# A hybrid decoder layer on one core: eight pairs of projection tiles by Strassen's form, attention's two chains side by side, first tiles by depth

## The chip, the cores and the metric

The kernel runs on one core of one Trainium2 chip. The metric is the device time in microseconds of one execution of the whole program; of several executions the median is given. One execution was recorded by the hardware profiler, and every row below is from it.

## The reference, cut to what matters

One layer over 1024 tokens of width 1024, all in 32-bit floats:

```python
h = rmsnorm(x, norm_in_g)
proj = h @ w_in            # 1024 x 4784, cut into eleven parts
(cq, ckv, kr, gate_mla, gq, gk, gv, gk_low, gate_gla, merge_a, merge_b) = split_in(proj)
...                        # latents cq (384) and ckv (256): rmsnorm, then queries, keys and values
o_mla = mla_attention(...) # 8 heads, causal softmax
y_a = (o_mla * silu(gate_mla)) @ w_mla_br
o_gla = gla_chunked(qg, kg, vg, log_a)   # 4 heads, a decaying state along the tokens
y_b = (rmsnorm(o_gla) * silu(gate_gla)) @ w_gla_br
merged = sigmoid(merge_a) * y_a + sigmoid(merge_b) * y_b
x = x + merged @ w_out
e = rmsnorm(p @ w_ple, ple_norm_g)
x = x + sigmoid(rmsnorm(x, ple_gate_norm_g) @ w_ple_gate) * e
out = rmsnorm(x, final_norm_g)
```

## The kernel before, in words

**Products.** Each 32-bit operand is cut into a high half that TensorE takes in its reduced format and a low half with the rest (`split`, lines 126 to 128: ScalarE writes the high half, VectorE the low one). One product is three matmuls, high by high, high by low and low by high (`mm3`, lines 144 to 147). A *bank* (`bank`, line 149) is one PSUM bank of 128 output features by 512 tokens: eight tiles of depth 128, three matmuls each, 24 matmuls of 512 columns; then an eviction scales it by the tokens' reciprocal norms `rb`.

**Streams.** `stream` (line 158) is a generator over weight tiles of 128 features. Each tile is loaded by SyncE into a slot, split, used for two banks (the two halves of the tokens), and dropped; the next tile is fetched when the first bank of the present one begins. All tiles of 128 by 1024 live in 35 slots, later 39, handed out in the order in which they became free.

**Order of the work.** The program is written as nested generators, and a scheduler orders each engine's instructions by the program's order and by which operands it expects to be ready; on the chip every engine runs its own list in order. The stages around the change:

1. *First tiles* (lines 298 to 350). The input comes transposed in eight tiles of depth (`xT`), is split into `xh` and `xl`, and squared for the norm. The mixed tile (`w0`: rotary keys and the low-rank gate) and four tiles of linear attention's queries and keys (`first`) are computed bank after bank. Six PSUM banks "d" and two "u" serve this stage. `rb` is known only after all eight tiles of the input.
2. *Values, gate and rotary tables.* Eight banks of values (`gv`), with the decay `bt` and the rotary tables `cs` and keys `krt` on VectorE and ScalarE beside them.
3. *Linear attention* (`gla(t, h)`, line 529) in four chains, two pairs of heads `t` by two halves of the tokens `h`. A chain has eleven steps: state updates (0), six levels of decay tiles with their cross products (1 to 6; `level`, line 533), the last level (7), the output (8), its norm (9), and the product with the gate (10). The chains run one after the other, and after every step one bank of `fill` is issued: a stream over 29 tiles of the projection, four of GLA's gate, four of MLA's gate, eight and eight of the merge gates, two and three of the latents. Its evictions scale (lines 466, 471), apply tanh and write to DRAM or keep the result.
4. *Latents and branch.* `finish_latent` (line 756) norms a latent: squares summed by TensorE, a Newton iteration of small VectorE operations, a broadcast by TensorE, scaling and splitting. The small latent is finished within `fill`, the large one later, and 16 half-size banks of the branch product `yb` fill around them, before the value products and softmax attention.
5. Softmax attention, output products, embedding and the final norm, which the change touches only where they read `krt` and `cs`.

## Time and profile before

| | us |
|---|---|
| time, median of three runs | 984.45 (983.88 to 986.28) |
| profiled execution, its own time | 983.49 |
| profiled execution, span from first to last instruction | 981.7 |
| TensorE busy in the span | 955.8 (5216 matmuls) |
| VectorE busy | 590.2 |
| ScalarE busy | 413.1 |
| GpSimd busy | 128.1 |

The span leaves out what lies before the first and after the last instruction. Busy times of the engines overlap. Matmuls are pipelined and their ends are modelled, so the distance between two starts, not the duration of one, is what a matmul costs in a stream. PE is TensorE, DVE VectorE, ACT ScalarE, POOL GpSimd, SP SyncE; L12 is line 12 of the program.

### The profile page before, as it was taken

What the parts mean: (1) busy time and instruction counts of PE and PEld (TensorE: products, weight loads), DVE (VectorE), ACT (ScalarE), POOL (GpSimd) and SP (SyncE); (2) the same over time, 40 slices, a digit from 0 to 9 for tenths busy, and PEclk for the clock granted to TensorE, in tenths of its full rate; (3) what the DMA queues carried; (4) which work ended last, traced back from release to release, by engine and by line L of the source; (5) the groups of instructions that cost most, each with busy time, mean ns of one, the idle gap of its engine ahead of it and who ended that gap; (6) DMA issues with size and microseconds to landing.
All of it is one profiled execution on the core that took longest, in us unless ns stands there. A gap on an engine that the chain in (4) does not pass through costs nothing.

```text
span 981.7 us, 14101 instructions
## 1 busy us (share of the span) xinstructions
PE 955.8 (97%) x5216; PEld 794.3 (81%) x5216; DVE 590.2 (60%) x1227; ACT 413.1 (42%) x800; POOL 128.1 (13%) x103
## 2 busy tenths in 40 slices
PE   7999999999999999999999999997999999999995
PEld 5887877887887887888888778886888788889985
DVE  6737765574474474433476469785757863239666
ACT  7306731331331342321333257676885432228333
POOL 2100000000000000001101012235363000000422
PEclk9999999999999999999999999997999999999998
DMA  7200211122222122211253844537146761136112
GB/s 281 94 22 22 65 43 43 57 84 86 76 108 86 63 79 86 97 65 43 82 181 127 230 121 121 133 98 177 49 147 229 254 208 65 49 119 188 53 69 103
DMA packets 47828, 105.70 MB, mean 108 GB/s; under 512 B 6736, under 2 KB 9616, under 8 KB 47760
## 3 DMA queue, kind: packets, MB, share of 16 engines
q1 hardware_dynamic: 47760, 104.81, 33.1%
q8 instruction: 41, 0.67, 0.3%
q14 instruction: 27, 0.22, 0.1%
HBM read 72.18 MB, written 25.20 MB: 99 GB/s over the span
## 4 chain that ended last, share of the span: by engine, by line
PE 86%; DVE 6%; ACT 3%; DMA 3%; issue 2%; SPq 0%; DVEq 0%; ACTq 0%
PE d L145 19%; PE d L147 18%; PE d L146 18%; PE pt L963 3%; PE pg L147 3%; PE pg L146 3%; PE pg L145 3%; PE L L559 2%; PE o L955 2%; PE s L146 2%; PE o L954 2%; PE s L147 2%; PE s L145 2%; PE o L690 1%; DMA kl<-kl 1%
## 5 line engine op out<-in xcount | busy, mean ns | idle before, releaser
L145 PE MATMUL d<-xh,wh 128*128 128x512 f32 x544 | 215.9, 400 | 2.8 <-ACT xh L132 2.6
L146 PE MATMUL d<-xl,wh 128*128 128x512 f32 x544 | 214.5, 395 | 0.1
L147 PE MATMUL d<-xh,wl 128*128 128x512 f32 x544 | 213.3, 393 | 0.1
L145 PEld LDWEIGHTS d<-xh,wh 128*128 128x128 f32 x544 | 103.0, 190 | 28.1 <-ACT xh L132 4.6
L127 ACT ACTIVATE wh<-wr 128x1024 fp32r<-128x1024 f32 (+4 forms) x81 | 76.2, 943 | 114.3 <-DMA wr<-in_w_in 40.4
L146 PEld LDWEIGHTS d<-xl,wh 128*128 128x128 f32 x544 | 103.0, 189 | 21.9 <-DVE xl L133 0.8
L147 PEld LDWEIGHTS d<-xh,wl 128*128 128x128 f32 x544 | 102.7, 189 | 21.9 <-DVE wl L128 0.5
L128 DVE TENSOR_TENSOR wl<-wr,wh 128x1024 fp32r<-128x1024 f32 (+2 forms) x59 | 74.6, 1267 | 71.2 <-ACT wh L127 71.1
L145 PE MATMUL pg<-wh,gh 128*128 128x256 f32 (+1 forms) x200 | 62.7, 314 | 0.0
L146 PE MATMUL pg<-wl,gh 128*128 128x256 f32 (+1 forms) x200 | 62.5, 313 | 0.0
L147 PE MATMUL pg<-wh,gl 128*128 128x256 f32 (+1 forms) x200 | 62.5, 313 | 0.0
L128 DVE TENSOR_TENSOR pt<-pt,pt 128x512 fp32r<-128x512 f32 (+1 forms) x96 | 51.4, 550 | 17.1 <-ACT pt L127 16.9
L494 ACT ACTIVATE z<-z 128x512 f32<-128x512 f32 x32 | 20.2, 631 | 98.0 <-DVE z L466 94.2
L924 ACT ACTIVATE p<-p,nm 128x128 f32<-128x128 f32 (+3 forms) x64 | 49.3, 772 | 21.2 <-DVE nm L914 21.1
L466 DVE TENSOR_TENSOR z<-d,rb 128x512 f32<-128x512 f32 x32 | 22.1, 690 | 51.3 <-PE d L147 51.3
L127 ACT ACTIVATE pt<-pt 128x512 fp32r<-128x512 f32 (+1 forms) x96 | 44.6, 485 | 15.5 <-PE pt L963 13.6
L145 PE MATMUL d<-mh,wh 128*128 128x512 f32 x128 | 50.7, 399 | 0.0
L146 PE MATMUL d<-ol,wh 128*128 128x512 f32 x128 | 50.1, 392 | 0.4 <-DVE ol L128 0.4
L147 PE MATMUL d<-mh,wl 128*128 128x512 f32 x128 | 50.2, 392 | 0.0
L147 PE MATMUL d<-oh,wh 128*128 128x512 f32 x128 | 50.1, 391 | 0.0
L146 PE MATMUL d<-ml,wh 128*128 128x512 f32 x128 | 49.9, 390 | 0.0
L145 PE MATMUL d<-oh,wh 128*128 128x512 f32 x128 | 49.9, 395 | 0.0
(263 smaller groups left out, 1924.4 us busy)
## 6 DMA issues: line engine op xcount, KB each, us to landing
wr<-in_w_in SPq DMA_DIRECT2D x33, 512.0 KB
d_ta<-z SPq DMA_DIRECT2D x16, 256.0 KB
d_tb<-z SPq DMA_DIRECT2D x16, 256.0 KB
tb<-d_tb SPq DMA_DIRECT2D x16, 256.0 KB
d_zb<-tb SPq DMA_DIRECT2D x16, 256.0 KB
d_e<-er SPq DMA_DIRECT2D x16, 256.0 KB
ta<-d_ta SPq DMA_DIRECT2D x16, 256.0 KB
zb<-d_zb SPq DMA_DIRECT2D x16, 256.0 KB
```

What stands on the lines that cost most here:

```text
L127: nc.scalar.activation(dst_hi, src, AF.Copy)
L128: (eng or nc.vector).tensor_tensor(dst_lo, src, f(dst_hi), op=ALU.subtract)
L145: nc.tensor.matmul(ps, lh, rh, start=first, stop=False)
L146: nc.tensor.matmul(ps, lh, rl, start=False, stop=False)
L147: nc.tensor.matmul(ps, ll, rh, start=False, stop=last)
L466: nc.vector.tensor_tensor(z, ps, rb[:, hs(h)], op=ALU.mult)
L494: nc.scalar.activation(z, z, AF.Tanh, scale=0.5)
L559: nc.tensor.matmul(L[:, hd * HALF + c * P : hd * HALF + (c + 1) * P], lt[rows(hd), cs], rt[rows(hd), cs], start=True, stop=True,)
L924: nc.scalar.activation(pt[:, :w], pt[:, :w], AF.Exp, bias=nm, scale=-1.0, accum_out=den)
L954: nc.tensor.matmul(po[:, n0:], vv, ts_[:, n0:HALF], start=kb == 0, stop=False)
L955: nc.tensor.matmul(po[:, n0:], vv, ts_[:, HALF + n0 : S], start=False, stop=kb == nk - 1)
L963: nc.tensor.transpose(pt[:, j * P : (j + 1) * P], pq[j][:, kb * P : (kb + 1) * P], ident)
```

## The change

**Pairs of tiles by a Strassen product** (the form with seven products and fifteen additions). 16 of the 29 tiles leave the stream: three of the first merge gate, all eight of the second, and the five latent tiles. They are taken in eight pairs. For a pair the weights are a 2 by 2 matrix of blocks (tile by half of the depth), the input another (half of the depth by half of the tokens). Seven products, each of four depth tiles and three matmuls of 512 columns, replace eight such. Sums of input blocks (`tq`) are made once, sums of weight blocks per pair on GpSimd, and the products are combined by accumulating twice into a bank and by additions on VectorE in the evictions. The input's four blocks now lie in tiles that hold high and low half side by side (`xq`).

**Linear attention's chains** run side by side: the two halves of pair 0 are one chain of 22 steps, those of pair 1 another, which starts seven steps later. In 29 rounds 22 banks of the remaining 13-tile stream are issued. One bank goes ahead of the rounds; the last three are issued in the next PSUM pool, around the input's sums.

**First tiles by depth.** The mixed tile and the two query tiles are computed together: each depth tile of the input goes into six open banks as it arrives. The PSUM pool has seven banks "d" and one "u" for it.

**Memory.** Rotary keys and tables and the finished gates are written to DRAM and loaded again later, the input is loaded a second time for its sums, slots are 34 and later 39, temporaries of 512 columns 8 instead of 6, linear attention's buffers 9 instead of 6. The small latent is finished after the pairs, ahead of the branch product. The DMA scratch of the program is set to 1024 bytes.

```diff
-NSLOT = 35
-NMORE = 4
-NTMP = 6
-NG = 6
+NSLOT = 34
+NMORE = 5
+NTMP = 8
+NG = 9
...
+        def mm3(ps, lh, ll, rh, rl, first, last, more=False):
+            nc.tensor.matmul(ps, lh, rh, start=first, stop=False, skip_group_check=more)
+            nc.tensor.matmul(ps, lh, rl, start=False, stop=False, skip_group_check=more)
+            nc.tensor.matmul(ps, ll, rh, start=False, stop=last, skip_group_check=more)
+        def pair(t):
+            return t[:, 0:HALF], t[:, HALF:S]
...
+        def strassen(get, jobs, xs, ahead=4):
+            raws, sums, ws, st = {}, {}, {}, {}
+            W = HALF
+            order = [(0, j) for j in (0, 4, 6, 1, 2, 3, 5)]
+            order += [(n, j) for n in range(1, len(jobs)) for j in range(7)]
+            def load(n):
+                if n < len(jobs):
+                    raws[n] = [alloc(F32, "wr") for _ in range(2)]
+                    for r, src in zip(raws[n], jobs[n][0]):
+                        nc.sync.dma_start(r, src)
+            def prep(q):
...
+                n, j = order[q]
+                r1, r2 = raws[n]
+                a11, a12, a21, a22 = r1[:, :W], r1[:, W:], r2[:, :W], r2[:, W:]
+                if j == 0:
+                    sums[n] = alloc(F32, "ws")
+                s1, s2 = sums[n][:, :W], sums[n][:, W:]
+                ws[n, j] = alloc(F32R, "sw")
+                if j == 0:
+                    nc.gpsimd.tensor_tensor(s1, a21, a22, op=ALU.add)
+                    nc.gpsimd.tensor_tensor(s2, s1, a11, op=ALU.subtract)
+                    nc.gpsimd.tensor_tensor(a21, a11, a21, op=ALU.subtract)
+                if j == 6:
+                    nc.gpsimd.tensor_tensor(a12, a12, s2, op=ALU.subtract)
+                split(*pair(ws[n, j]), (a11, s2, s1, a21, a12, a22, a12)[j])
+                if q % 7 == 5:
+                    drop(raws[n][n > 0])
+                    load(n + 1)
+                if q % 7 == 6:
+                    drop(*raws.pop(n), sums.pop(n))
+            def run(n, j):
+                b = ("abcbadc" if n else "abcbydx")[j]
+                first = b not in st
+                if first:
+                    st[b] = get("w", "w" + b)
+                hi, lo = pair(ws[n, j])
+                for i in range(4):
+                    c = slice(i * P, (i + 1) * P)
+                    mm3(st[b], hi[:, c], lo[:, c], *pair(xs[j][i]), first and i == 0, i == 3, b in "abc")
+                drop(ws.pop((n, j)))
+                _, ev1, ev2 = jobs[n]
+                def plus(t, b):
+                    nc.vector.tensor_tensor(t, st[b], t, op=ALU.add)
+                if j == 0:
+                    st["e"] = t2("e")
+                    nc.scalar.activation(st["e"], st["a"], AF.Copy)
+                elif j == 1:
+                    st["v"] = t2("v")
+                    nc.vector.tensor_tensor(st["v"], st["b"], st["e"], op=ALU.add)
+                elif j == 3:
+                    w_, z = t2("w"), t2("z22")
+                    st["u"] = w_
+                    nc.vector.tensor_tensor(w_, st["b"], st["e"], op=ALU.add)
+                    nc.vector.tensor_tensor(z, st["c"], w_, op=ALU.add)
+                    ev2(1, z)
+                    if not n:
+                        plus(st["v"], "c")
+                        plus(st["v"], "x")
+                        ev1(1, st["v"])
+                elif j == 4:
+                    if n:
+                        ev1(0, st["a"])
+                    else:
+                        z = t2("z11")
+                        nc.vector.tensor_tensor(z, st["y"], st["e"], op=ALU.add)
+                        ev1(0, z)
+                elif j == 5:
+                    plus(st["u"], "d")
+                    ev2(0, st["u"])
+                elif j == 6 and n:
+                    plus(st["v"], "c")
+                    ev1(1, st["v"])
+                if j == order[7 * n + 6][1]:
+                    st.clear()
...
+            for q, (n, j) in enumerate(order):
+                prep(q + ahead)
+                run(n, j)
...
-            get = psum_pool({"d": (HALF, 6), "u": (HALF, 2)}, ps0)
+            get = psum_pool({"d": (HALF, 7), "u": (HALF, 1)}, ps0)
...
+            w3 = [(alloc(F32, "wr"), alloc(F32R, "wh"), alloc(F32R, "wl")) for _ in range(3)]
+            src3 = [a["w_misc"][:, NVEC : NVEC + S]] + [job(W_GQ + t, None)[0] for t in range(2)]
+            ev3 = [ev_misc, ev_q(0), ev_q(1)]
+            ps3 = [[None, None] for _ in range(3)]
+            def load3(n, c0, c1):
+                raw, hi, lo = w3[n]
+                c = slice(c0, c1)
+                if n == 0 and c0 == 0:
+                    split(hi[:, c], lo[:, c], wm0[:, NVEC : NVEC + c1])
                 else:
+                    nc.sync.dma_start(raw[:, c], src3[n][:, c])
+                    split(hi[:, c], lo[:, c], raw[:, c])
+                if c1 == S:
+                    drop(raw)
...
+            for k in range(8):
+                t = alloc(F32, "xT")
+                for c in (hs(0), hs(1)) if k == 0 else (slice(0, S),):
+                    nc.sync.dma_start(t[:, c], a["xT"][k * P : (k + 1) * P, c])
+                if k == 0:
+                    load3(0, 0, P)
+                for h in range(2):
+                    xq[h].append(alloc(F32R, f"x{h}{k}"))
+                    split_gain(*xin(k, h), t[:, hs(h)], col(V_IN + k))
+                xT.append(t)
+                if k == 0:
+                    load3(0, P, S)
+                    load3(1, 0, 256)
+                    load3(2, 0, 256)
+                if 0 < k < 3:
+                    load3(k, 256, S)
+                if k == 2:
+                    nc.sync.dma_start(ident, a["cst"][:, C_ID : C_ID + P])
+                for n in range(3):
+                    _, hi, lo = w3[n]
+                    for h in range(2):
+                        if k == 0:
+                            ps3[n][h] = get("d", "d")
+                        c = slice(k * P, (k + 1) * P)
+                        mm3(ps3[n][h], hi[:, c], lo[:, c], *xin(k, h), k == 0, k == 7)
+                if k:
+                    square(k - 1)
...
+                nc.sync.dma_start(d_krt, f(krt))
+                for y in range(2):
+                    nc.sync.dma_start(d_cs[y], cs[y])
+                drop(ang, kk, kr, krt, *cs)
...
-                for _ in range(2):
+                for _ in range(2 if tb < 3 else 1):
...
-            jobs += [job(W_MA + m, ev_t(d_ta[m])) for m in range(8)]
-            jobs += [job(W_MB + m, ev_t(d_tb[m])) for m in range(8)]
-            fill = stream(get, jobs, xh, xl)
+            jobs += [job(W_MA + m, ev_t(d_ta[m])) for m in range(5)]
+            order = [(n, h) for n in range(12) for h in range(2)] + [(12, 1), (12, 0)]
+            fill = stream(get_fill, jobs, xin, order=order)
             next(fill)
-            def steps():
+            def chain(t):
                 for h in range(2):
-                    for t in range(2):
-                        yield from gla(t, h)
+                    yield from gla(t, h)
             next(fill)
-            n_left = 2 * len(jobs) - 5
-            for _ in steps():
-                next(fill)
-                n_left -= 1
-            drop(*bt, gci)
+            def load_x(i):
+                raw[i] = [alloc(F32, "xr") for _ in range(2)]
+                for n in range(2):
+                    nc.sync.dma_start(raw[i][n], a["xT"][(i + 4 * n) * P : (i + 4 * n + 1) * P, :])
+            def keep(t):
+                for m in (2 * t, 2 * t + 1):
+                    nc.sync.dma_start(d_sg[m], sg[m])
+                    drop(sg[m])
+                drop(bt[t])
+            one, two, lag = chain(0), chain(1), 7
+            for n in range(22 + lag):
+                if n < 22:
+                    next(one)
+                if n >= lag:
+                    next(two)
+                if n not in (8, 10, 12, 14, 17, 20, 23):
+                    next(fill)
+                if n == 22:
+                    keep(0)
+                    load_x(0)
+                    load_x(1)
...
+        with tc.tile_pool(name="psS", bufs=1, space=PSUM) as psS:
+            get = psum_pool({"d": (HALF, 4), "w": (HALF, 4)}, psS)
+            getF[0] = get
...
+            ts = [tile_of(W_MA + m, ev_t(d_ta[m])) for m in range(5, 8)]
+            ts += [tile_of(W_MB, ev_t(d_tb[0]))]
+            ts += [tile_of(W_CKV + j, ev_ckv(j)) for j in range(2)]
+            ts += [tile_of(W_CQ + j, ev_cq(j)) for j in range(3)]
+            ts += [tile_of(W_MB + m, ev_t(d_tb[m])) for m in range(1, 8)]
+            jobs = [((p_[0], q_[0]), p_[1], q_[1]) for p_, q_ in zip(ts[::2], ts[1::2])]
+            tq = [[], [], [], []]
+            def operand_sums(i):
+                r = raw.pop(i)
+                for n in range(2):
+                    nc.scalar.activation(r[n], r[n], AF.Copy, scale=col(V_IN + i + 4 * n))
+                x11, x12, x21, x22 = (r[n][:, hs(h)] for n in range(2) for h in range(2))
+                for q_ in tq:
+                    q_.append(alloc(F32R, "tq"))
+                nc.gpsimd.tensor_tensor(x11, x12, x11, op=ALU.subtract)
+                nc.vector.tensor_tensor(x12, x22, x12, op=ALU.subtract)
+                nc.gpsimd.tensor_tensor(x22, x22, x11, op=ALU.subtract)
+                nc.vector.tensor_tensor(x21, x21, x22, op=ALU.subtract)
+                for q_, x in zip(tq, (x11, x22, x12, x21)):
+                    split(*pair(q_[i]), x)
+                drop(*r)
+            load_x(2)
+            load_x(3)
+            keep(1)
+            xs = [xq[0][:4], tq[1], tq[0], tq[2], xq[0][4:], tq[3], xq[1][4:]]
+            pairs = strassen(get, jobs, xs)
+            next(fill)
+            operand_sums(0)
+            operand_sums(1)
+            next(fill)
+            operand_sums(2)
+            next(fill)
+            next(pairs)
+            operand_sums(3)
+            drop(*xq[1][:4])
+            next(pairs)
+            for _ in fill:
+                pass
+            for q in range(7 * len(jobs)):
+                next(pairs)
+                j = q - 7 * (len(jobs) - 1)
+                if j >= 0:
+                    drop(*xs[j])
+                if j == 3:
+                    sg = [alloc(F32, f"sg{m}") for m in range(4)]
+                    oh, ol = [], []
+                    for m in range(4):
+                        nc.sync.dma_start(sg[m], d_sg[m])
+                        oh.append(alloc(F32R, "oh"))
+                        ol.append(alloc(F32R, "ol"))
+                        split(oh[m], ol[m], sg[m])
+                        drop(sg[m])
+            drop(rb)
...
-            for n in range(n_left - 5):
-                next(fill)
-            kvh, kvl = finish_latent(get, "u", "L", "ckv", 256, V_KV)
-            next(fill)
-            next(fill)
-            next(fill)
+            kvh, kvl = finish_latent(get, "d", "d", "ckv", 256, V_KV)
...
+            cs = [alloc(F32, "cs") for _ in range(2)]
+            for y in range(2):
+                nc.sync.dma_start(cs[y], d_cs[y])
...
-                    nc.sync.dma_start(f(qk[nm, 2 * pr][64:96]), f(krt[32 * y : 32 * y + 32]))
+                    nc.sync.dma_start(f(qk[nm, 2 * pr][64:96]), d_krt[32 * y : 32 * y + 32])
```

## Rows read from the trace of the kernel before

**Rows 1.** The page's busy times, and TensorE's busy tenths in 40 slices:

```profile
PE 955.8 (97%) x5216; PEld 794.3 (81%) x5216; DVE 590.2 (60%) x1227; ACT 413.1 (42%) x800; POOL 128.1 (13%) x103
...
PE   7999999999999999999999999997999999999995
```

**Rows 2.** The page's chain that ended last, shares by engine:

```profile
PE 86%; DVE 6%; ACT 3%; DMA 3%; issue 2%; SPq 0%; DVEq 0%; ACTq 0%
```

**Rows 3.** Timeline, evictions of two neighbouring banks (start, us, instruction, idle before):

```profile
426.93 0.69 DVE L466 TENSOR_TENSOR z<-d,rb 128x512 f32<-128x512 f32 x1 [2.66 <-PE d L147]
...
432.37 0.69 DVE L466 TENSOR_TENSOR z<-d,rb 128x512 f32<-128x512 f32 x1 [4.75 <-PE d L147]
```

**Rows 4.** Chain of waits in linear attention (start us, us, what):

```profile
129.12 1.09 PE L L559 x16
...
148.37 1.09 PE L L559 x16
155.12 1.09 PE L L559 x16
```

**Rows 5.** Timeline of TensorE at the start, then busy time of that stretch:

```profile
7.65 0.63 PE L147 MATMUL d<-xh,wl 128*128 128x512 f32 x1
10.39 1.22 PE L145 MATMUL d<-xh,wh 128*128 128x512 f32 x2 [2.12 <-ACT xh L132]
...
15.93 0.39 PE L147 MATMUL d<-xh,wl 128*128 128x512 f32 x1
...
4.80:15.70 10.90, 8.50 (x17) 5.42 (x18) 7.32 (x7) 8.72 (x10) 0.00 (x0) 1.00 0.99 375
```

**Rows 6.** Timeline of ScalarE, first half of the scale row:

```profile
47.05 0.60 ACT L342 ACTIVATE rb<-rb 128x512 f32<-128x512 f32 x1 [2.00 <-PE rb L243]
```

**Rows 7.** Groups by line, 118 to 418 us (busy us, mean ns, idle before):

```profile
L128 DVE TENSOR_TENSOR wl<-wr,wh 128x1024 fp32r<-128x1024 f32 x24 | 29.4, 1224 | 30.7 <-ACT wh L127 30.5
L466 DVE TENSOR_TENSOR z<-d,rb 128x512 f32<-128x512 f32 x29 | 20.0, 690 | 43.9 <-PE d L147 43.9
...
L145 PE MATMUL d<-xh,wh 128*128 128x512 f32 x362 | 144.3, 399 | 0.0
```

**Rows 8.** Stretches: busy us (instructions) of PE, PEld, DVE, ACT, POOL; clock, DMA, GB/s:

```profile
118.00:418.00 300.00, 300.00 (x1891) 242.90 (x1889) 164.81 (x308) 93.14 (x188) 12.13 (x16) 1.00 0.21 75
...
200.00:220.00 20.00, 20.00 (x155) 16.15 (x154) 17.96 (x41) 7.62 (x14) 0.83 (x1) 1.00 0.18 66
...
425.00:459.00 34.00, 34.00 (x152) 28.16 (x151) 5.88 (x8) 5.91 (x8) 2.57 (x2) 1.00 0.14 50
672.00:688.00 16.00, 9.81 (x38) 8.70 (x37) 7.49 (x26) 8.81 (x21) 8.54 (x5) 0.58 0.73 190
688.00:704.00 16.00, 16.00 (x92) 13.77 (x91) 11.97 (x33) 12.49 (x28) 4.13 (x4) 1.00 0.12 43
```

**Rows 9.** Timeline of VectorE before the first cross products, fourth level's differences:

```profile
119.83 0.41 DVE L546 TENSOR_TENSOR r<-b 128x256 f32<-128x256 f32 x1
```

**Rows 10.** Timeline of VectorE and GpSimd near 912 us:

```profile
911.54 0.48 DVE L1186 SCALAR_TENSOR_TENSOR x<-et,re,x 128x256 f32<-128x256 f32 x1
...
912.70 1.29 POOL L1216 TENSOR_TENSOR x<-x,fg 128x512 f32<-128x512 f32 x1 [149.00 <-ACT g L1188]
...
912.82 1.46 DVE L1186 SCALAR_TENSOR_TENSOR x<-et,re,x 128x256 f32<-128x256 f32 x1
```

**Rows 11.** Timeline of ScalarE at the stall of 672 us:

```profile
676.00 1.06 ACT L127 ACTIVATE wh<-wr 128x1024 fp32r<-128x1024 f32 x1 [3.63 <-DMA wr<-in_pT]
```

**Rows 12.** Chain of waits and timeline, the two latents, first and last:

```profile
459.53 1.68 PE ss L222 x16
...
475.19 1.28 DVE L128 TENSOR_TENSOR cl<-latents,ch 128x512 fp32r<-128x512 f32 x2
...
495.01 1.68 PE ss L222 x16
...
519.45 0.39 PE L145 MATMUL d<-ch,wh 128*128 128x512 f32 x1
```

126 lines of the change are left out of this document (57 added, 69 removed).

## The prediction, made before the changed kernel ran

> **What bounds the kernel now.** I read the page's busy times and slices first. TensorE has work in 955.8 of 981.7 us, and its slices are full except the first, one near 670 us and the last [rows 1]; the chain that ended last is 86% TensorE [rows 2]. So what counts is the number of matmul steps and the few places where TensorE waits. The timeline gives the step: two neighbouring banks of the input projection are evicted 5.44 us apart (426.93, 432.37) [rows 3], and a bank is 24 matmuls of 512 columns, so 0.2267 us each. In linear attention the chain of waits repeats every 6.75 us (148.37, 155.12): one bank and 1.31 us for one step's own products [rows 4]. TensorE is full there, VectorE has 164.8 of 300 us [rows 8]. The profiled execution took 983.49 us, 0.96 below the median; I sum against it and add 0.96.
>
> **The change, part by part.**
>
> *Strassen.* 16 of the 29 streamed tiles go in 8 pairs. Before, a pair is 4 banks, 4 x 5.44 = 21.76 us. After, 7 products of 12 matmuls, 7 x 2.72 = 19.04 us. The matmuls keep their form (128x128 weights, 512 columns, new weights each time), so I price them by the same step: 8 x 2.72 = **21.8 us less**. What hides the additions: per pair VectorE gets 7 low halves of 512 columns (0.69 each, as an eviction of that size [rows 3]) and nine operations on the products' sums (five additions, four scalings), 16 x 0.69 = 11.0 us, where two tiles now cost two splits of 1.22 and four evictions, 5.2 [rows 7]; ScalarE gets 7 high halves, a copy and four activations, 12 x 0.60 = 7.2 [rows 6]; GpSimd four weight sums of 1.29 us [rows 10], 5.2. All lie inside 19.04 us of TensorE, in a stretch in which VectorE now works 5.9 of 34 us [rows 8]. GpSimd slows VectorE: while one of its operations runs, a VectorE operation that takes 0.48 takes 1.46 us [rows 10]; even 11.0 + 5.2 fits. It adds one kind of wait: banks a, b and c are accumulated into a second time, and the first of those matmuls waits until VectorE or ScalarE has read the first sum, which it has one product (2.72 us) or more to do. Behind that matmul stand all later products on TensorE, and behind those the evictions; a reader that is late by one GpSimd operation costs up to 1. From 0 to 8 us over 8 pairs, I take **1**, since the cover is wide.
>
> The Trainium skill (TensorE: Matmul & The Clock Gate, section Back-to-back issue gap) gives about 131 ns a matmul for a sustained stream of weight loads and matmuls of 512 columns. By it the 96 matmuls would be 12.6 us and the total some 9 us higher; the row's 226.7 ns differs, and decides.
>
> *Entry.* Four operand sums, each over two input tiles: ScalarE 8 scalings x 1.06 and 16 high halves x 0.60, 18.1 us [rows 6, 11]; of 16 differences and 16 low halves 24 on VectorE, 24 x 0.69 = 16.6, and 8 on GpSimd, 8 x 1.29 = 10.3, during which VectorE can be held. With three evictions and four weight parts (7 x 0.69 = 4.8) VectorE may need 31.7 us. The cover is three banks (16.3) and the three first products, which need no sum (8.2): 24.5. So 0 (part done under the last steps of attention, or on time) to 7.2 us late; I take **2**, because load and first two sums can start under five banks of attention's tail. The saves of finished gates (four of them, two tiles per chain) wait on SyncE for VectorE's last gate product; queued behind them are the input's reload and the next tile's weights, due two banks (10.9 us) later, so a wait of that size is free.
>
> *Attention's two chains.* Before, 44 steps each carry a bank; after, 29 rounds carry 22 banks, up to two steps each, and rounds 8, 10, 12, 14, 17, 20, 23 carry none. No TensorE work is added; cover is lost. Per chain of 11 steps (four of them before): TensorE 300 us less 1086/24 = 45.25 banks (362 matmuls in each of three lines [rows 7]) x 5.44 = 53.8, so 13.5; VectorE 164.8 less the stream's own 71.6 (24 splits of 1.22, 29 evictions of 0.69, and for 16 banks of gates two such operations each) = 93.2, so 23.3 [rows 7, 8]. The tightest stretch is rounds 8 to 17: the first chain is in steps 8 to 10 and 0 to 6 of its next half, the second in steps 1 to 10, 20 of the 22 steps of two such chains, with five banks. VectorE: 20/22 x 46.6 + 5 x (2 x 0.69 + 0.61) = 52.4. TensorE: 24.5 + 27.2 = 51.7. VectorE becomes the equal of TensorE. For it speaks that decay tiles are made far ahead (the fourth level's differences end at 120.2, the first level's products run at 129.12) [rows 4, 9], and buffers for that rise from 6 to 9. Bounds: 0, and VectorE at its densest share now, 17.96 of 20 [rows 8]: 52.4/0.90 - 51.7 = 6.5. I take **3**.
>
> *First tiles by depth.* Now TensorE starts at 4.82 us, pauses 2.12 until the second input tile (10.39), and matmuls last 0.63 until about 15.7, 0.39 after [rows 5]: it ran the lower of its levels, 1.2 GHz, though the granted clock reads 1.00. 17 matmuls are done by then where 48 steps of 0.2267 would fit. New: each input tile feeds 18 matmuls instead of 6, so the pause shrinks and, with steadier work, the full level should come earlier. Bounds: all 31 matmuls, 7.0 us gained; or 2 us lost, if the first scale row, which lands at 47.05 [rows 6], comes later while seven of seven banks are full. Six banks were full then already with 0.2 us of wait. I take **3 gained**, near half of the gain possible. The gate products share one bank instead of two; they lie beside 43 us of value products.
>
> *Exit.* Both latents are finished after the last product instead of one after the other. From the first sum of squares to the last low half is 17.0 us for the small (459.53 to 476.5), and 24.4 for the large up to its first use (495.01 to 519.45) [rows 12]. In line 41.4 us; cover: six banks of the branch product (16.3), two sums, 48 value products (10.9), 30.6. So 0 to 11 us; ten later branch banks can fill in, I take **3**. Gates split again in the last pair (4 x 1.22) fit its missing preparations.
>
> *Spills.* Rotary tables, keys' rotary part and gates go to DRAM and back, the input is read again: some 12 MB of 105.7, into stretches whose DMA share is now 0.21 and 0.14 [rows 8]. Nothing.
>
> *The stall at 672.* ScalarE waited 3.63 us with a weight split for a late load [rows 11]; everything behind it stopped, and in 16 us TensorE made 38 matmuls, then 92, its granted clock at 0.58, so partly at 1.2 GHz [rows 8]: 54/92 x 16 = 9.4 us. The change frees other slots at other times; it may go or return. Bounds -9.4 and +9.4, I take 0.
>
> Sum: -21.8 - 3 + 1 + 2 + 3 + 3 = -15.8; 983.5 - 15.8 = 967.7, as a median **968.7 us**.
>
> **Rivals.**
> *The stall at 672 goes too*: 983.5 - 15.8 - 9.4, median 959. For: slots of the resident keys and tables are free earlier. Against: nothing aims at it.
> *One more such stall appears* (a queue head waits for a load): 978. For: every load in it is placed by slot order; against: only one occurred before.
> *Entry and exit are paid in full*: -24.8 + 1 + 3 + 7.2 + 11 = -2.6, median 982. For: VectorE's sums above; against: fillers are at hand.
> *Slower: attention starves.* In rounds without a bank TensorE waits for VectorE (6.5 us), and the pauses are long enough that the clock falls as at 672, 9.4 us each. With two falls: -24.8 + 6 + 6.5 + 18.8 = +6.5, median 991; it decides from the second fall on. Against: decay tiles run ahead.
> *It does not do what it says*: if sums changing bank made a product's matmul step 0.259 instead of 0.227, all is given back: about 987 with the losses but without gain at the start, 984 with it. Against: steps are even now across changes of bank.
>
> **How the numbers follow.** Forecast 0.57 (own range 962 to 975), stall gone 0.13, new stall 0.12, entry and exit 0.09, starving 0.06, longer step 0.03. A measurement tells 0.3%, 3 us, so faster is below 981.5. Faster: 0.57 + 0.13 + 0.11 + 0.03 = 0.84; same: 0.01 + 0.06 + 0.01 + 0.02 = 0.10; slower 0.06. Range 957 to 982, which leaves the lower half of the second case and most of the last ones out.
>
> **What would show it.** Right: 96 fewer long matmuls, product stretches of 2.72 us without gaps, steps of 0.227, TensorE full between 130 and 300 us. Wrong: idle of TensorE behind VectorE in attention with the granted clock under 1, or a gap where products begin or end; VectorE near 9 tenths in attention would mean that it, not TensorE, sets that stretch.

## The result

The changed kernel takes 998.4 us (994.3 to 999.28, 4 runs), the kernel before beside it 985.37: ratio 1.0119 [1.0079, 1.0159], so 1.2% slower. Forecast were 968.7 us and a range of 957 to 982: the sign was wrong. The profiled execution took 999.28 us, its span is 997.5.

The page of the changed kernel (busy us, share of the span, instructions; TensorE's busy tenths in 40 slices; shares of the chain that ended last), beside [rows 1, 2]:

```profile
PE 949.3 (95%) x5120; PEld 788.9 (79%) x5120; DVE 664.4 (67%) x1342; ACT 453.3 (45%) x881; POOL 189.8 (19%) x143
...
PE   8999899997999899999989999897999999999996
...
PE 53%; DVE 7%; DMA 5%; ACT 1%; issue 1%; SPq 1%; POOL 1%; DVEq 0%; POOLq 0%; ACTq 0%
```

The 96 matmuls are gone (5216 to 5120). TensorE is busy 6.5 us less over a span that is 15.8 us longer, and slices that were full before now show 8 and 7 among the nines.

Stretches of the changed kernel (as in [rows 8]: us, then busy us and instructions of PE, PEld, DVE, ACT, POOL; clock, DMA, GB/s):

```profile
130.00:215.00 85.00, 85.00 (x510) 68.59 (x510) 55.22 (x97) 30.38 (x55) 3.43 (x3) 1.00 0.26 84
215.00:245.00 30.00, 23.97 (x261) 20.48 (x261) 24.81 (x49) 10.36 (x32) 1.68 (x4) 0.91 0.06 19
245.00:305.00 60.00, 57.09 (x429) 45.40 (x429) 43.78 (x90) 22.30 (x46) 10.88 (x9) 0.96 0.37 125
305.00:335.20 30.20, 25.41 (x117) 20.49 (x115) 19.70 (x36) 17.32 (x39) 13.13 (x9) 1.00 0.40 145
335.20:490.20 155.00, 155.00 (x693) 128.73 (x694) 105.90 (x157) 59.23 (x99) 49.44 (x35) 0.99 0.30 100
...
672.00:688.00 16.00, 14.05 (x81) 11.75 (x79) 9.84 (x25) 8.46 (x16) 3.99 (x3) 1.00 0.62 164
680.00:700.00 20.00, 14.68 (x65) 12.15 (x64) 11.10 (x34) 13.29 (x30) 9.44 (x5) 0.76 0.77 201
```

From 215 to 335 us TensorE idles 13.7 us; while the pairs run (335.2 to 490.2) it never does. The stall at 672 only moved, to 680 to 700. Two of the waits in attention, on TensorE's timeline (the bracket tells the idle time before and what ended it):

```profile
227.49 1.16 PE L705 MATMUL L<-r 64*128 64x128 f32 x16 [2.57 <-DVE at L787]
...
240.43 2.08 PE L705 MATMUL L<-r 64*128 64x128 f32 x16 [2.46 <-DVE os L848]
```

Landmarks tell where the 15.8 us lie (us from the start of the span). "gv ends" is the end of the last product of the values, "first of pairs" the first matmul into a bank wa (empty where there are no pairs), "projections" the end of the last matmul of the input projection, "scores" the first score matmul, "output" the first matmul of the output product. The runs e1 to e18 are explained below:

| kernel | gv ends | first of pairs | projections | scores | output | span |
|---|---|---|---|---|---|---|
| before | 115.8 | | 489.6 | 549.1 | 787.0 | 981.7 |
| changed | 114.6 | 335.2 | 496.9 | 555.8 | 803.4 | 997.5 |
| e1 squares | 115.9 | 340.4 | 501.4 | 560.9 | 806.4 | 1000.5 |
| e2 no pairs | 114.4 | | 490.5 | 558.3 | 807.9 | 1002.5 |
| e5 six pairs | 114.1 | 362.2 | 483.5 | 545.6 | 790.8 | 984.9 |
| e8 start alone | 115.1 | | 490.1 | 551.6 | 792.0 | 987.1 |
| e10 spill alone | 115.7 | | 496.5 | 557.0 | 803.3 | 997.6 |
| e13 rows back | 115.6 | 333.6 | 495.3 | 555.5 | 795.1 | 989.4 |
| e14 rows back, six | 114.4 | 364.2 | 485.5 | 550.4 | 787.0 | 981.3 |
| e15 and few buffers | 115.5 | 359.7 | 481.0 | 545.0 | 782.1 | 976.3 |
| e16 rows back, seven | 115.0 | 340.4 | 482.3 | 543.0 | 781.2 | 975.4 |

Some work lies on the other side of a landmark in the changed kernel, and I count it where the kernels compare. The kernel before has the small latent's 16 sums and 4 broadcasts (2.63 us) ahead of its last projection. The changed kernel has, between its first pair and its last projection, 32 sums for the latents (3.23 us) and 17 matmuls of the branch product (3.85 us).

From the kernel before to the changed one, then:

- Start: -1.2.
- **Attention and entry: +23.5.** The kernel before needs 373.8 us from gv to the last projection; without 32 banks of 5.44 us (174.1) and the 2.6 us that is 197.1. The changed kernel takes 220.6 to its first pair.
- **Pairs: -19.4.** 161.74 - 3.23 - 3.85 = 154.7 us against 174.1.
- Exit: +3.8, from the last projection to the scores, 58.9 + 7.1 against 59.5 + 2.6.
- **Softmax attention: +9.7**, from scores to output, 247.6 against 237.9.
- The rest: -0.6. Sum +15.8.

The 23.5 are 16.2 us of idle TensorE (2.5 at 118 to 122, 8.9 from 215 to 305, 4.8 at the entry) and, as the remainder, some 7.3 us of slower matmuls: behind waits of 1.8 to 2.5 us, at 124, 242 and 287 us, some 25 long matmuls last about 0.63 us and not 0.39, and the granted clock from 215 to 245 and from 245 to 305 us is 0.91 and 0.96. VectorE's timeline in the changed kernel shows late evictions (start, us, instruction, idle before and its releaser):

```profile
202.03 0.69 DVE L615 SCALAR_TENSOR_TENSOR z<-d,rb 128x512 f32<-128x512 f32 x1 [2.01 <-PE d L148]
...
239.00 1.28 DVE L848 TENSOR_TENSOR os<-o,os 128x512 f32<-128x512 f32 x2
...
240.80 1.28 DVE L615 SCALAR_TENSOR_TENSOR z<-d,rb 128x512 f32<-128x512 f32 x2
...
243.51 0.69 DVE L615 SCALAR_TENSOR_TENSOR z<-d,rb 128x512 f32<-128x512 f32 x1
```

The three banks that are read from 240.80 on were finished at 207.9, 213.8 and 220.5 us. While all three "d" banks are full, no fill can be issued, and the chains' small products are all that TensorE has. The entry, on TensorE's timeline:

```profile
330.02 0.39 PE L148 MATMUL d<-x,wl 128*128 128x512 f32 x1
335.19 0.69 PE L146 MATMUL wa<-x,sw 128*128 128x512 f32 x1 [4.79 <-ACT sw L127]
```

### The profile page after: what moved, and what is told of

Its sections match the earlier page's. It is cut to its first block, busy times and chain, and to the rows that moved or that the text cites. A ratio compares the mean times of both kernels' runs of the same rounds, so it can differ in the third digit from the quotient of the medians.

```text
span 997.5 us, 14178 instructions
## 1 busy us (share of the span) xinstructions
PE 949.3 (95%) x5120; PEld 788.9 (79%) x5120; DVE 664.4 (67%) x1342; ACT 453.3 (45%) x881; POOL 189.8 (19%) x143
## 4 chain that ended last, share of the span: by engine, by line
PE 53%; DVE 7%; DMA 5%; ACT 1%; issue 1%; SPq 1%; POOL 1%; DVEq 0%; POOLq 0%; ACTq 0%
PE d L148 5%; PE d L147 5%; PE d L146 5%; PE pg L146 3%; PE pg L148 3%; PE pg L147 3%; PE pt L1185 3%; PE s L147 2%; PE o L1177 1%; PE wb L148 1%; PE wb L146 1%; PE wb L147 1%; DMA kl<-kl 1%; PE wa L146 1%; PE s L148 1%; PE wa L147 1%
## 5 line engine op out<-in xcount | busy, mean ns | idle before, releaser
L146 PE MATMUL d<-x,wh 128*128 128x512 f32 x288 | 116.9, 409 | 3.5 <-ACT x L132 1.5
L148 PE MATMUL d<-x,wl 128*128 128x512 f32 x288 | 114.3, 400 | 1.8 <-DVE wl L128 1.8
L147 PE MATMUL d<-x,wh 128*128 128x512 f32 x288 | 115.7, 402 | 0.0
L127 ACT ACTIVATE wh<-wr 128x1024 fp32r<-128x1024 f32 (+6 forms) x67 | 59.3, 892 | 91.5 <-PE d L147 15.8
L128 DVE TENSOR_TENSOR wl<-wr,wh 128x1024 fp32r<-128x1024 f32 (+4 forms) x45 | 51.7, 1151 | 39.9 <-ACT wh L127 36.1
L146 PEld LDWEIGHTS d<-x,wh 128*128 128x128 f32 x288 | 55.8, 194 | 18.3 <-ACT x L132 2.7
L148 PEld LDWEIGHTS d<-x,wl 128*128 128x128 f32 x288 | 55.6, 193 | 14.2 <-DVE wl L128 2.0
L147 PEld LDWEIGHTS d<-x,wh 128*128 128x128 f32 x288 | 55.9, 194 | 11.3 <-issue 0.2
L1438 POOL TENSOR_TENSOR x<-x,fg 128x512 f32<-128x512 f32 x16 | 20.6, 1290 | 191.7 <-DMA et<-d_e 149.6
L127 ACT ACTIVATE sw<-wr 128x512 fp32r<-128x512 f32 x40 | 24.9, 630 | 50.8 <-PE wb L148 18.6
```

The lines of the kernel that those rows point to most:

```text
L127: nc.scalar.activation(dst_hi, src, AF.Copy)
L128: (eng or nc.vector).tensor_tensor(dst_lo, src, f(dst_hi), op=ALU.subtract)
L146: nc.tensor.matmul(ps, lh, rh, start=first, stop=False, skip_group_check=more)
L147: nc.tensor.matmul(ps, lh, rl, start=False, stop=False, skip_group_check=more)
L148: nc.tensor.matmul(ps, ll, rh, start=False, stop=last, skip_group_check=more)
L1438: nc.gpsimd.tensor_tensor(xo, xo, fg[:, hs(h)], op=ALU.mult)
```

## Experiments: attention

I had three theories at first. **A**: the evictions and the chains' squares take buffers of one tag, which are handed out in program order, so a bank waits for a buffer that comes behind the squares of a late chain. **B**: VectorE has no more room. **C**: the loss comes from the operand sums, which were pulled into attention, and from the entry.

**e1** gives the squares another place:

```diff
-                    junk = t2("junk")
+                    junk = at[:, hs(hd)]
```

> The only edit: in the chain's last-but-two step the squares of its output go into the score tile, which is dead by then, and no longer take one of the eight temporaries that the evictions of the filling banks take too. Theory A (the loss in attention comes from temporaries handed out in program order: banks finished at 207.9 to 220.5 us are evicted at 240.8 to 243.5 only, because their temporary comes behind the squares of a chain that is late): the gap from a finished bank to its eviction falls from 20 to 33 us to under 8, TensorE's stretch 220 to 243 is no longer idle, the first Strassen product begins at 312 to 322 us in place of 335.2, and the whole is 976 to 988 us. Theory B (VectorE has no more room in this stage, 52.4 of 53 us whatever the order): the first product begins at 330 to 336 us, the whole takes 994 to 1000 us. Theory C (the operand sums pulled into attention and the wait for the first weights' split are the loss): as B.

1007.1 us, ratio to before 1.0221 [1.0189, 1.0252]: worse than the change, and outside what any of the three expected. The first half of theory A held: evictions follow their banks, and TensorE works 59.5 of the 60 us from 220 to 280 (53.1 in the changed kernel). Then it stops. TensorE's timeline of e1:

```profile
292.65 1.16 PE L705 MATMUL L<-r 64*128 64x128 f32 x16 [2.25 <-DVE nt L306]
299.79 1.23 PE L836 MATMUL o<-gqkv,at 64*128 64x128 f32 x8 [5.08 <-DVE at L787]
315.33 0.80 PE L146 MATMUL d<-x,wh 128*128 128x512 f32 x1 [8.87 <-ACT wh L127]
```

Its fill has run out: the weights of the next tile leave SyncE's queue only at 308.33, behind a load for the pairs and a save of gates:

```profile
301.70 0.33 SPq L210 DMA_DIRECT2D wr<-in_w_in  x1
305.71 0.33 SPq L893 DMA_DIRECT2D d_sg<-sg  x1
308.33 0.33 SPq L137 DMA_DIRECT2D wr<-in_w_in  x1
```

The first pair begins at 340.4, later than in the changed kernel. So the time does not hang on the late evictions; the idle time moved. Theory A falls.

**e2** is e1 with all 29 tiles as plain fill (the edit in short):

```diff
-jobs += [job(W_MA + m, ev_t(d_ta[m])) for m in range(5)]
+jobs += [... all of W_MA, W_MB, W_CKV, W_CQ ...]
-pairs = strassen(get, jobs, xs)
+for q, _ in enumerate(fill):
```

> The edit of the run before (squares into the dead score tile), and with it all 29 tiles stream as plain fill with 24 products each: no pairs, no operand sums, no Strassen; the chains stay seven steps apart, and the first tiles by depth stay. If the arithmetic of the pairs holds as it was reckoned (96 products of 0.2267 us, 21.8, less 4 to 8 us for its entry and exit), the projections end 14 to 22 us later than in the run before and so does the kernel. If the pairs bring nothing because the stage is held by other engines, the two are within 4 us. Against the kernel before the change this one has only the start and the chains' order: theory A expects it between 980 and 992 us, theory B 995 to 1015.

999.3 us, 1.0145 [1.0112, 1.0179]. The projections end at 490.5 us, 10.9 earlier than e1 and not 14 to 22 later: with chains seven steps apart and enough fill TensorE is busy without a gap from 160 to 490 us.

```profile
160.00:490.00 330.00, 330.00 (x1933) 270.99 (x1933) 152.44 (x279) 92.74 (x188) 17.80 (x19) 1.00 0.26 89
```

(Behind 490 this run is not comparable: it finishes the key latents with nothing beside them.) So the chains' arrangement by itself costs little, 376.2 us from gv to the last projection against 373.8 in the kernel before; taking fill away from it costs much. e2 still hands out no bank in the same seven rounds; it is the scheduler that pulls later banks forward, 27.3 of them ahead of the chains' end where e1 has 24.0.

**e3** (ScalarE copies each bank, VectorE scales the copy) and **e4** (no additions for the operand sums):

```diff
-                nc.vector.tensor_tensor(z, ps, rb[:, hs(h)], op=ALU.mult)
+                nc.scalar.activation(z, ps, AF.Copy)
+                nc.vector.tensor_tensor(z, z, rb[:, hs(h)], op=ALU.mult)
```

> The changed kernel, but in the attention stage ScalarE copies each finished bank into the temporary, and VectorE then scales it there, without reading the bank. Temporaries are shared as before. Theory A (the temporary comes late): no help, the copy waits for the same temporary; first Strassen product at 332 to 340 us, whole 996 to 1003 us. Theory B (VectorE's reading of the banks is too much for it): banks come free earlier, the first product begins 4 to 12 us earlier, the whole takes 986 to 994 us.

999.35 us, 1.0137 [1.0111, 1.0164], first pair at 334.5: no gain. This does not settle theory B, since the copy takes the same late temporaries; e5 does, below, where VectorE is as busy and TensorE is full.

```diff
-                nc.gpsimd.tensor_tensor(x11, x12, x11, op=ALU.subtract)
-                nc.vector.tensor_tensor(x12, x22, x12, op=ALU.subtract)
-                nc.gpsimd.tensor_tensor(x22, x22, x11, op=ALU.subtract)
-                nc.vector.tensor_tensor(x21, x21, x22, op=ALU.subtract)
```

> The changed kernel without the four additions for each operand sum (16 in all, on GpSimd and VectorE): the Strassen products take the scaled input blocks in their place, so their values are not those of the projection. Copies, splits and all products stay. Theory A: the first Strassen product begins within 3 us of 335.2 and the whole is 994 to 1000 us. Theory C (the sums are the loss, by GpSimd's port on VectorE and by the entry): the first product begins 6 to 16 us earlier, the whole is 982 to 992 us.

993.7 us, 1.0077 [1.0049, 1.0104]; the first pair begins at 329.2, six us earlier than in the changed kernel, and the wait there is 0.72 in place of 4.79; the whole stays above the 982 to 992 us of theory C. It holds for the entry and for little more: the waits at 229 and 243 us, 2.72 and 2.45, are still there.

What e1 and e2 say together is theory **D**: 26 banks are too few to cover the 29 rounds of the chains. e5 to e7 put pairs back into plain fill; e5 is the change with

```diff
-                if n not in (8, 10, 12, 14, 17, 20, 23):
-                    next(fill)
+                next(fill)
```

and 17 tiles of fill in place of 13, 12 in pairs in place of 16.

> The changed kernel with 12 tiles in pairs in place of 16, so that 17 tiles stream as fill and every round of the chains has a bank (34 banks in place of 26); squares and evictions share their temporaries as in the changed kernel. Theory D (attention is as long as its two chains, which ended between 317 and 329 us in all kernels run so far, also where TensorE was full; with 26 banks there is too little for TensorE until then, and what it lacks shows as idle time wherever a buffer or a load happens to be late): the four extra tiles (8 banks of 5.44 us, 43.5) fill most of the 16.2 us idle and 9 us of slow clock, the first Strassen product begins at 352 to 362 us, not at 335.2 + 43.5 = 378.7, the six pairs take 123 us, the projections end at 475 to 485 us (496.9 before this edit) and the whole takes 977 to 987 us. Theory A (the temporaries' order alone): the banks are evicted as late as before, the stretch 215 to 300 keeps 12 to 16 us idle, the first product begins at 368 to 380 us, the whole takes 1000 to 1008 us (four pairs' tiles at full price).

986.2 us, 1.0004 [0.9974, 1.0034]: 12 us less than the changed kernel, though two pairs' saving (5.4 us) is given up, and inside D's range; its first pair, at 362.2, is at the range's edge. Stretches of e5:

```profile
215.00:245.00 30.00, 30.00 (x262) 24.97 (x260) 22.39 (x41) 8.37 (x15) 1.67 (x4) 1.00 0.21 70
245.00:305.00 60.00, 58.96 (x416) 46.98 (x415) 46.08 (x92) 26.47 (x65) 14.38 (x10) 1.00 0.30 96
```

TensorE is full again but for 1.0 us, at a clock of 1.00, with the temporaries shared as in the changed kernel and VectorE as busy (22.4 and 46.1 us, against 24.8 and 43.8). The six pairs take 121.3 us, of which 114.3 are 42 products of 2.72: their arithmetic holds. **e6**, e5 with e1's edit:

> The run before and the squares in the dead score tile. Theory D: within 4 us of the run before, since neither is short of work, or up to 6 us better where an eviction was late there. Theory A: 14 to 22 us better than the run before.

987.5 us, 1.0012 [0.9988, 1.0037], as D expects. **e7**, 14 tiles in pairs (three rounds without a bank), with e1's edit:

> 14 tiles in pairs, 15 as fill (30 banks, three rounds without one), and the squares in the dead score tile. Theory D: between the changed kernel and six pairs in idle time (2 to 8 us left in 130 to 340), first product at 333 to 345 us, projections end 475 to 488 us, whole 977 to 990 us. If instead every fewer pair costs its 12 products (2.7 us) and nothing comes back: 1010 us (e1 plus one pair).

988.7 us, 1.0051 [1.002, 1.0082], within D's bounds. **e9** takes the fill away from the chains (eight banks ahead, the rest behind):

```diff
+            for n in range(7):
+                next(fill)
             for n in range(22 + lag):
...
-                if n not in (8, 10, 12, 14, 17, 20, 23):
-                    next(fill)
```

> The changed kernel with the two chains of attention almost by themselves: eight banks of fill (the gates) ahead of them, none handed out beside them, the other 18 behind them. Measures the chains' own length. Theory D (the chains' own steps set the length, not TensorE): first state product at 155 to 165 us, and from there to the end of the last transposes (oT) 190 to 210 us, as long as with 22 banks among them (208 us, from 115 to 323.6, in the changed kernel). If instead the chains are slow only because their products queue behind banks of 5.44 us on TensorE, they take 110 to 150 us here.

1021.9 us, 1.0362 [1.0324, 1.0401], from two runs. The chains were not as alone as meant: their first state product comes at 115.37 and not at 155 to 165, and the matmuls of 14 banks lie among them. From there to the last transposes (288.98) it is 173.6 us, between the two expectations. e9 from 150 to the end of the chains:

```profile
150.00:289.00 139.00, 112.29 (x933) 93.17 (x932) 99.04 (x217) 47.70 (x124) 18.21 (x18) 0.89 0.19 63
```

TensorE idles 26.7 of 139 us, so the chains have a length of their own even where TensorE is free. But that length is not the 190 to 210 us of theory D: with 14 banks the stage is 173.6 us, with 24 to 28 it is 200 to 215. D is right that fill is short, wrong that the chains alone set the length.

Counting the long matmuls up to the chains' end gives the balance, from the end of gv to the last transposes:

| kernel | us | banks | us of the banks | left |
|---|---|---|---|---|
| e1 | 212.7 | 24.0 | 130.6 | 82.1 |
| changed | 209.0 | 24.8 | 134.9 | 74.1 |
| e18 (below) | 213.9 | 25.7 | 139.6 | 74.2 |
| e2 | 208.6 | 27.3 | 148.3 | 60.3 |
| e16 (below) | 212.1 | 27.8 | 151.0 | 61.1 |
| e5 | 231.5 | 31.0 | 168.4 | 63.0 |
| before, one chain at a time | 302.5 | 45.5 | 247.3 | 55.2 |

So with 27 banks or more some 61 us are left for the chains' own products (59 to 65 in all such runs but e11 and e12, below, which have 73 and 74), and with 24 to 26 banks 70 to 82: 9 to 21 us are lost, in whichever place. A rival for part of it stays untested: the reload of the input, the pairs' weights and the saves of gates stand in SyncE's queue among the fill's weights, which is what held e1 at 308 us, and no run with eight pairs moves those loads alone. e6 and e7 keep them where they are, with e1's edit, and TensorE idles at most 2.2 us from 150 us to the chains' end there (17.7 in e1); so more fill is enough, but another order of the loads may help too.

**e18** keeps all 16 tiles in pairs and gives the chains six temporaries as before the change (`NG = 6`), on top of e13 (below):

> All 16 tiles in pairs as in the changed kernel, six temporaries for the chains, keys' rows from on-chip memory (e13 with fewer buffers). Theory D (26 banks are too few for 208 us of chains): TensorE still lacks 8 to 16 us at 200 to 335, first product at 328 to 336 us, whole 985 to 992 us. If the extra buffers were the reason in attention: first product at 315 to 324 us, whole 974 to 981 us.

994.8 us, 1.0099 [1.0074, 1.0125]; first pair at 335.1. The first pair is where D expects it, the whole 2.8 us above D's range and far from the other one: the extra buffers are not the reason. Stretches of e18:

```profile
215.00:245.00 30.00, 26.41 (x239) 23.96 (x236) 22.38 (x46) 8.49 (x28) 1.79 (x4) 0.77 0.06 19
245.00:305.00 60.00, 55.98 (x404) 44.62 (x404) 47.49 (x98) 24.53 (x51) 11.22 (x10) 0.97 0.30 106
```

Its longest waits in the first of them, on TensorE's timeline:

```profile
226.75 1.16 PE L705 MATMUL L<-rq,rk 64*128 64x128 f32 x16 [1.01 <-DVE rq L812]
230.49 2.08 PE L705 MATMUL L<-r 64*128 64x128 f32 x16 [2.58 <-DVE r L695]
```

## Experiments: start and softmax attention

**e8** is the kernel before with the first tiles by depth and nothing else of the change.

> The kernel before with the first part of the change alone: misc and the two query tiles accumulate by depth from block 0 (seven banks for outputs, one for the sums), everything behind gv as before. The start gained 1.2 us in the changed kernel where 3 was forecast. Expected: gv ends at 114 to 116 us (115.8), and the whole is 1 to 3 us under the kernel before; if the start only moves VectorE's and ScalarE's work into the beginning of the fill (the 2.4 us wait at 118 to 122 us that the changed kernel and all its variants show), the fill starts 2.4 us late here too and the whole is within 1.5 us of the kernel before.

988.4 us, 1.0034 [1.0009, 1.0059], above both expectations. gv ends 0.7 us earlier; the fill's first weights are 1.4 us late at 116 to 119; and the scores, which stand in unchanged code, begin with a wait of 2.92 us for a query copy. This part alone brings no gain.

**e10** is the kernel before with the spill of the rotary tables alone (the lines of the change):

```diff
+                nc.sync.dma_start(d_krt, f(krt))
+                for y in range(2):
+                    nc.sync.dma_start(d_cs[y], cs[y])
+                drop(ang, kk, kr, krt, *cs)
...
-                    nc.sync.dma_start(f(qk[nm, 2 * pr][64:96]), f(krt[32 * y : 32 * y + 32]))
+                    nc.sync.dma_start(f(qk[nm, 2 * pr][64:96]), d_krt[32 * y : 32 * y + 32])
```

> The kernel before with one part of the change: the key's rotary table and the two cosine and sine tables go out to memory behind the rope step and come back ahead of the softmax attention, whose copies of the key's rotary rows then come from memory. From the first scores to the output product the changed kernel takes 247.6 us, the kernel before 237.9. If these reloads are the reason: 244 to 250 us for that stage here and 990 to 997 us in all. If the stage's length only follows how its instructions fall in order (theory E; the start alone, which touches nothing there, already has 240.4): 236 to 243 us and a whole within 4 us of the kernel before.

999.1 us, 1.0135 [1.0113, 1.0158], above the expected 990 to 997: this part alone costs as much as the whole change. It costs in two places. At 117 to 124 us TensorE waits 5.0 us, most of it for ScalarE at the chains' first products, and the projections end 6.9 us later:

```profile
117.35 1.09 PE L593 MATMUL U<-gqkv,kdT 128*64 128x128 f32 x16 [1.23 <-ACT kdT L587]
121.79 2.08 PE L566 MATMUL L<-r 64*128 64x128 f32 x16 [3.35 <-ACT r L554]
```

And the softmax attention takes 246.3 us. One row each of the stretch from first score to output product, the kernel before, e8, e10 and the changed kernel:

```profile
549.10:787.00 237.90, 228.39 (x1222) 193.13 (x1223) 175.96 (x435) 154.51 (x343) 75.50 (x54) 0.97 0.51 153
```

```profile
551.60:792.00 240.40, 231.13 (x1223) 195.66 (x1224) 175.15 (x435) 154.39 (x343) 75.14 (x54) 0.96 0.50 150
```

```profile
557.00:803.30 246.30, 232.82 (x1223) 195.80 (x1224) 175.40 (x434) 155.83 (x342) 74.35 (x54) 0.97 0.49 149
```

```profile
555.80:803.40 247.60, 234.25 (x1224) 197.19 (x1225) 178.13 (x437) 157.04 (x343) 74.32 (x54) 0.96 0.50 150
```

The matmuls are the same, and so is the traffic (149 to 153 GB/s). In e10 TensorE has 4.0 us more of idle time and 4.4 more of busy time for them. What differs is the order in which the scheduler (the expectations call it the planner) wrote them: from the first score to the last embedding product TensorE's list is the same in the kernel before and in e8, and another one in e10 and in the changed kernel, with waits before value products that neither of the first two has. In e10:

```profile
761.56 0.50 PE L964 MATMUL o<-pt,vp 128*128 128x512 f32 x1 [1.80 <-ACT pt L127]
762.48 0.50 PE L965 MATMUL o<-pt,vp 128*128 128x512 f32 x1 [0.42 <-DVE pt L128]
```

With two more of 0.69 and 0.50 us at 624 and 627 us these are 3.4 us that end behind ScalarE or VectorE and have no counterpart in the kernel before. The waits inside the stage that end behind copies, with the stall near 690 us, sum to 8.4 us in e10 and, with its stall near 678, to 7.8 in the kernel before. So the idle time grew where the order is new, not at the copies; the 4.4 us of busy time are not explained.

**e13** keeps the saves and the reload and takes away the copies from memory: in the changed kernel, the table comes back on chip ahead of the stage, and the copies start from there.

```diff
+            krt = alloc(F32R, "krt")
+            nc.sync.dma_start(f(krt), d_krt)
...
-                    nc.sync.dma_start(f(qk[nm, 2 * pr][64:96]), d_krt[32 * y : 32 * y + 32])
+                    nc.sync.dma_start(f(qk[nm, 2 * pr][64:96]), f(krt[32 * y : 32 * y + 32]))
```

> The changed kernel (16 tiles in pairs), but the keys' rotary table comes back from memory into on-chip memory ahead of the softmax attention, and the copies into each head's keys start from there, as in the kernel before. TensorE's order from the first scores to the last embedding product is then again that of the kernel before, row for row. Theory F (the copies from memory made the planner write another order, and that order costs the time): first scores to output product 237 to 241 us (247.6), whole 988 to 992 us. Theory G (the traffic through memory itself costs it): 244 to 249 us, whole 995 to 1000 us.

991.2 us, 1.0058 [1.0033, 1.0084]; the stage takes 239.6 us. Its row:

```profile
555.50:795.10 239.60, 230.39 (x1222) 194.58 (x1223) 176.73 (x438) 154.59 (x343) 75.36 (x54) 0.96 0.51 154
```

The saves and reloads stay, TensorE's order is that of the kernel before again, and 8.0 of the 9.7 us are back with it. This is theory F, with one reservation: the new order and the copies from memory come and go together in these runs, and only the waits above speak for the order.

## Experiments: a better version

**e14** is e5 with e13's edit.

> The same with 12 tiles in pairs and a bank of fill in each round (e5). Theories D and F together: the two repairs add up, 986.2 - 6 to 8 us: 977 to 981 us, under the kernel before; first scores to output product 237 to 241 us (245.2 in e5). Theory G: 984 to 988 us.

984.0 us, 0.9975 [0.9953, 0.9997], over the expected 977 to 981: the softmax stage takes 236.6 us, 8.6 less than in e5, but from projections to scores it is 2.8 us more, and the projections end 2.0 us later. **e15**, e14 with six temporaries for the chains:

> The run before with six temporaries for the chains, as before the change, in place of nine: the chains can't run so far ahead on VectorE while the rope tables are still to be made (at 107 to 124 us their level steps stood between the rope steps). Expected: the fill's first weights' split no longer waits (0.6 + 1.9 us idle at 117 to 122 us in e5), 1 to 3 us better than the run before; if the chains, two at a time, need the buffers, TensorE is idle at 200 to 300 us instead and the run is 3 to 10 us worse.

979.7 us, 0.9946 [0.9923, 0.9969], 4.3 us better than e14 and so a little more than expected. But the wait at 118 to 122 us is still 2.1 us, so the reason given for it is wrong; two smaller waits of e14 in attention (1.77 at 147 us, 0.92 at 298) are gone. **e16**, e13 with 14 tiles in pairs and three rounds without a bank:

> As e14 with 14 tiles in pairs and three rounds without a bank. A pair less in plain fill saves 2.7 us (12 products of 0.2267); theory D expects that 30 banks leave 2 to 10 us idle in 200 to 345, so the run is between 2 us better and 6 us worse than e14: 976 to 987 us.

980.8 us, 0.9947 [0.9926, 0.9967], inside the range, though the expected 2 to 10 us of idle time did not appear. Stretches of e16:

```profile
215.00:245.00 30.00, 30.00 (x262) 25.02 (x260) 20.98 (x40) 8.11 (x13) 1.68 (x4) 1.00 0.21 71
245.00:305.00 60.00, 60.00 (x470) 48.44 (x471) 48.58 (x98) 28.00 (x68) 12.32 (x10) 1.00 0.30 108
```

With two tiles more in the fill than e13 no gap is left there. **e17** has both edits, 14 tiles in pairs and six temporaries:

> Both together: 14 tiles in pairs and six temporaries for the chains, keys' rows from on-chip memory. If the two gains of e15 and e16 over e14 (4.3 and 3.2 us) are separate, 976 to 979 us; if both only fill the same idle time, 979 to 982 us. Either way under the kernel before and the changed one.

983.9 us, 0.9983 [0.9963, 1.0004], above both expected ranges: the gains don't add, and two waits of 0.83 and 1.29 us stand in attention and one of 3.18 at the entry. **e11** (six pairs, rope steps two beside every gv tile, key latents inside the last pair) and **e12** (and tables reloaded there):

> Six pairs (squares and evictions share temporaries), and two small moves: two steps of the rope tables beside every gv tile again, so that VectorE has done them when the fill's first weights come; and the key latents are finished after the third product of the last pair, not behind all pairs. Expected from the rows of the six pairs: the wait of 0.6 + 1.9 us at 117 to 122 us goes, and the wait of 2.3 us at 499.9 us (rb behind VectorE); first scores at 539 to 543 us (545.6), whole 979 to 984 us. If the stage behind (245 us from first scores to the output product) gives it back: 985 to 988 us.

> The run before, and the cosine and sine tables come back during the last pair in place of behind all pairs, ahead of the gate tiles on SP's queue. Expected: the wait of 2.6 us at the first scores (for a key tile's copy) falls under 1 us, 1 to 2 us better than the run before; if that wait comes from the rotary rows of the keys, which stay as they are, no difference.

994.1 us, 1.0088 [1.0056, 1.012], and 1000.0, 1.0134 [1.0112, 1.0157]: both expectations missed. In both, early products of the chains now wait 6.4, 1.7 to 1.9 and 4.0 to 4.8 us at 118 to 141 us; e12's projections end 4.7 us after e11's, with a wait of 2.35 us for a branch weight at 490.5.

e15 and e16 beat both kernels: the kernel before by 0.5%, with intervals that lie below 1, and the changed one, by the two ratios to the kernel before (0.9947 / 1.0119 = 0.983), by 1.7%.

## Why the prediction was wrong, step by step

- *Strassen* (-21.8, +1): right. TensorE has no gap in 155.0 us, and a product takes 2.72 us; measured are -19.4. The pairs' 154.7 us are 2.4 more than 56 products of 2.72, most of it at the beginning, where behind the entry's wait eight matmuls last about 0.63 us and not 0.39. That the pairs' matmuls take 0.2267 us agrees with [rows 3]. It does not agree with the 131 ns that the prediction quotes from the Trainium skill (TensorE: Matmul & The Clock Gate, section Back-to-back issue gap).
- *Attention's two chains* (+3, bounds 0 to 6.5) and *entry* (+2): the step that failed. Together they measure 23.5 us. The working compared sums of busy time in a stretch, 51.7 us for TensorE and 52.4 for VectorE, and charged the difference, as if one of the two would be full. The rows show that neither is: from 215 to 245 us TensorE works 24.0 and VectorE 24.8 of 30 us, from 245 to 305 they work 57.1 and 43.8 of 60. TensorE waits for single steps of the chains (2.57 and 2.46 us behind VectorE) with no bank to run meanwhile, and its granted clock falls to 0.91. This is the sign of being wrong that the prediction names. The rival "attention starves" had this mechanism, with a chance of 0.06 and 991 us; its price for the clock, two falls of 9.4 us, was too high, since all slower matmuls together are some 7.3. e5 against the changed kernel, and e16 against e13, put banks back in place of pairs and bring TensorE's time back, so the lack of fill decides. The entry's own wait, 4.79 us, lies inside its bounds (0 to 7.2).
- *Spills* ("Nothing"): the second failed step. They were weighed as traffic, and the traffic is near what was reckoned (11.0 MB more). But e10 shows 13 us for the rotary tables alone, 8.4 of them in the softmax attention. e13 shows that 8.0 us go with the copies from memory and the order written around them, not with the saves and reloads. The working had no term for a list that is written anew.
- *First tiles by depth* (-3): 1.2 gained at gv's end; behind it stands the wait of 2.5 us at 118 to 122, and e8 alone is 0.3% slower. TensorE does reach its higher level earlier (matmuls last 0.39 us and not 0.63 from 12.40 us on, not from about 15.7 [rows 5]), but it waits 1.24 us for the input at 6.75 all the same.
- *Exit* (+3, 0 to 11): 3.8. *Stall at 672* (0): it came later with the stage and stayed, 5.3 us idle.
- One sum among the rivals is off: with the pairs' saving all given back, the terms -3 + 1 + 2 + 3 + 3 give a median of about 990 us, 993 without the gain at the start, and not 984 and 987. It bears on the chances, not on the forecast.

From -15.8 to +15.8 are 31.6 us: attention with its entry 18.5, softmax attention 9.7, start 1.8, pairs 1.4, exit 0.8, the rest -0.6. The first two carry 28.2.

Three things stay open: which single coupling of the chains sets the 174 us of e9; why TensorE waits at 118 to 122 us in the versions with chains seven steps apart (e15 took away the buffers, and it stayed); and how the softmax stage's loss divides between the new order and the copies from memory.

## What to carry over

Work that fills another stage's waits is worth more than its own length. Before taking it away, compare the stage's length without fill with the fill that is left, and treat equal loads of two engines as a loss. Here, shrinking the saving from eight pairs to seven or six gave more than it cost. Where a scheduler writes the order, a change of where a small table lies can rewrite a whole later stage, so test each convenience (a spill, a buffer count) alone.

## What the runs showed of the hardware

TensorE's granted clock fell in stretches that have short waits only. In e18 it is 0.77 from 215 to 245 us, and the longest waits there are 1.01 and 2.58 us; from 224.6 to 244.5 us TensorE has only products of 128 columns; e5 and e16, without waits there, show 1.00.
